# Norm steps and sums of squares on another engine, pool waits by tile, and the norm's row one half block later, in a two-layer decoder trunk

## The chip, the cores and the metric

The kernel runs on one core of one Trainium2 chip. The metric is the device time of one execution in microseconds (us), the median of several runs. The engines are TensorE (PE; PEld is its weight load), VectorE (DVE), ScalarE (ACT), GpSimd (POOL) and SyncE (SP), whose queue issues most loads. SBUF is the memory that all of them work in; PSUM holds what PE accumulates.

## The reference

One sequence of 512 tokens with a width of 1024, in float32, passes two layers. Each layer is a half SwiGLU block, a token mixer and another half SwiGLU block, every one behind an RMS norm and added to the residual:

```
h = h + 0.5 * swiglu(rmsnorm(h, ffn_norm_a[i]), ...)      # hidden width 2816
h = h + mixer_i(rmsnorm(h, mix_norm[i]))                  # layer 0: MLA, layer 1: NSA
h = h + 0.5 * swiglu(rmsnorm(h, ffn_norm_b[i]), ...)
rmsnorm(x, g) = x * rsqrt(mean(x * x) + 1e-6) * g
swiglu(x)     = (silu(x @ w_gate) * (x @ w_up)) @ w_down
```

MLA is multi-head latent attention with 16 heads; NSA is sparse attention with a compressed, a selected and a window branch. A final norm follows. What matters here is the norm: a sum of squares over the 1024 channels for each token, its inverse root, and a product.

## The kernel before

**Layout.** The residual lies in SBUF as eight tiles `h[c]` of 128 channels by 512 tokens. Every matmul is made of three in fp32r, on a high and a low part of both operands: ACT copies the high part, DVE subtracts to get the low part (`split`, L165 to L174; `wslab`, L132 to L155, for weights: L143 the copy, L145 the subtraction on DVE, L149 the subtraction on POOL inside the mixers' attention). Weights pass through two raw buffers (`wr`) and two split ones.

**The norm.** As a chunk of `h` is finished, `norm_chunk` splits it, scaled by the gain only, and `sumsq` (L246) squares it on ACT (L250) and adds the square to `s2` (L254, on POOL). The inverse root is applied late, to the results: `norm_col` (L273) lets PE sum `s2` over the partitions into a column of 128x4 (`pc`, L278) and `rsqrt` (L256) takes its inverse root: three preparing steps on DVE (L259 to L261) and three Newton iterations, of four operations on POOL with `pool=True` (L264 to L267) or of three on DVE without (L269 to L271). `norm_bcast` (L286) spreads the column over all partitions with eight small matmuls (`pb`, L290), and ACT copies that to `row`. The last two chunks ahead of an FFN are kept in `late`; their squares are added inside the FFN. The first FFN takes its sums from a second copy of x, by token (`squares`).

**An FFN** (`ffn`, L368), four of them, works on 22 blocks of 128 hidden channels. The first three (`PLAIN`) are plain matmuls: a gate half (`plain(.., 0, ..)`) and an up half (`plain(.., 1, ..)`) of 48 matmuls of 256 columns each. Their gates need `row`, which is made after the second block: `norm_bcast`, the copy, then `gate` (L374) and `act` for blocks 0 and 1, ahead of the third block's matmuls in the program. `gate` multiplies by `row` on DVE (L377), takes Silu on ACT (L378) and multiplies again (L379). The blocks from 3 on use Strassen's scheme, seven products in place of eight, with sums of weights (`wsums`, on DVE and ACT) and of inputs (`combine`, L224: y on ACT, L236 to L238 and a split on DVE), four combines in each FFN. The products go to `px`, `pq` and `pg` in PSUM; `down` products of the three blocks before are put between them (`unit`). The last four blocks' down product runs chunk by chunk and feeds the next norm.

**The mixers** (`mla`, L641; `nsa`, L833) project, run a software pipeline over tiles of scores (`attend`) and end in an output projection (`w_o`, `po`), whose second half feeds the next norm chunk by chunk. NSA opens further pools on the way: "cmp" for its compressed branch, then "nsat".

**What sets the order.** The framework places semaphores and works out at compile time a fixed order for each engine, from the program's order and from when it expects operands to be ready; every engine's queue then runs in that order. Pools of tiles are stacked in SBUF. An FFN's pools ("act", "ft") and a mixer's pools land on bytes of pools that were released before. By default everything in such a pool waits for every user of those released pools.

Of the kernel before, what the change touches and what calls it, by code (L numbers as in the profile page):

```python
# [15 lines left out]
ALU = mybir.AluOpType  # L16
# [4 lines left out]
D = 1024  # L21
# [40 lines left out]
class Kern:  # L62
# [183 lines left out]
    def sumsq(self, t, first=False):  # L246

        nc = self.nc
        sq = self.sp.tile([P, S], F32, tag="s2", bufs=2, name="s2") if first else self.scratch("sq")
        nc.scalar.activation(sq, t, AF.Square)  # L250
        if first:
            self.s2 = sq
        else:
            nc.gpsimd.tensor_tensor(self.s2, self.s2, sq, op=ALU.add)  # L254

    def rsqrt(self, y, v, t, psum, n, pool):  # L256

# [110 lines left out]
    def ffn(self, idx, gain_next, ap, tp):  # L368
        nc, a = self.nc, self.a
# [4 lines left out]
        def gate(f, g):  # L374

            t = tg[f] = tp.tile([P, S], F32, tag="tg", bufs=2, name="tg")
            nc.vector.tensor_tensor(t, g, row, op=ALU.mult)  # L377
            nc.scalar.activation(t, t, AF.Silu, scale=-1.0)  # L378
            nc.vector.tensor_tensor(t, t, row, op=ALU.mult)  # L379
# [4 lines left out]
        def act(f):  # L384
            t = tu[f]
            if f < PLAIN:
                t = tu_tile()
                nc.vector.scalar_tensor_tensor(t, tu[f], -1.0, tg[f], op0=ALU.mult, op1=ALU.mult)
            else:
                nc.vector.tensor_tensor(t, t, tg[f], op=ALU.mult)  # L390
            ah[f] = ap.tile([P, S], F32R, tag="act", bufs=4 * NG, name="ah")
            al[f] = ap.tile([P, S], F32R, tag="act", bufs=4 * NG, name="al")
            self.split(t, ah[f], al[f])
# [19 lines left out]
        sums, xts = self.small_sums, []  # L413

        def tokens(t):

            xts.append(tp.tile([P, D], F32, tag="fr", bufs=3, name="xt"))
            with self.tc.issue_after(self.high.ins):
                nc.scalar.dma_start(xts[t], a["x_tok"][t * P : (t + 1) * P, :])

        def squares(t):
            nc.scalar.activation(xts[t], xts[t], AF.Square, accum_out=sums[:, t : t + 1])
# [7 lines left out]
        for f, g in enumerate(gates):  # L430
            u = tu[f] = self.bank(("mm", "S")[f % 2], "pu")
            self.plain(idx, f, 0, g)
            if f == 1 and idx == 0:

                squares(0)
                tokens(3)
                squares(1)
            self.plain(idx, f, 1, u)
            if f == 0:
                for c in self.late:  # L440
                    self.sumsq(self.h[c])
                col = self.norm_col(D, self.s2, pool=True) if idx else None
            elif f == 1:
                if idx == 0:
                    squares(2)
                    squares(3)
                    col = self.rsqrt_col(sums, D, pool=True)
                pb = self.norm_bcast(col)
                row = tp.tile([P, S], F32, tag="row", bufs=1, name="row")
                nc.scalar.activation(row, pb, AF.Copy)  # L450
                for e in range(2):
                    gate(e, gates[e])
                    act(e)
            else:
                gate(f, g)
                act(f)
            for p in (((0,), (1,), (2, 3)) if idx else ((0, 1), (2,), (3,)))[f]:
                self.combine(p)
# [182 lines left out]
    def mla(self, gain_next):  # L641
        nc, tc, a = self.nc, self.tc, self.a
        with ExitStack() as cx:
            mp = cx.enter_context(tc.tile_pool(name="mla", bufs=1))
            tp = cx.enter_context(tc.tile_pool(name="mlat", bufs=2))
            self.chain, self.chained = None, True
            self.scr = tp, "p", 6
            cst = mp.tile([P, S], F32, name="cst")
# [184 lines left out]
    def nsa(self, gain_next):  # L833
        nc, tc, a = self.nc, self.tc, self.a
        with ExitStack() as cx:
            mp = cx.enter_context(tc.tile_pool(name="nsa", bufs=1))
            qp = cx.enter_context(tc.tile_pool(name="nsaq", bufs=1))
            rvalid = self.gains[:, 53:57]
            gat = mp.tile([P, 4, 3 * H], F32, name="gat")
            gcmp = mp.tile([P, 4, H], F32, name="gcmp")  # L840
# [91 lines left out]

            ks, vs, qs, pc, th, bank = {}, {}, [], {}, {}, {}

            with tc.tile_pool(name="cmp", bufs=1) as bp:
                self.chain, self.chained = None, True
                bt = self.bias_table(bp)
                for t in vcm:
# [39 lines left out]
                col = self.norm_col(D, self.s2)  # L978
# [36 lines left out]
                    nc.scalar.activation(gat[:, j, :], pv[j][:, 256:VG], AF.Sigmoid, scale=col[:, j : j + 1])  # L1015
                nc.vector.tensor_tensor(gcmp, gat[:, :, 0 : 3 * H : 3], rvalid[:, :, None].to_broadcast([P, 4, H]), op=ALU.mult)

            tp = cx.enter_context(tc.tile_pool(name="nsat", bufs=2))

            pths, ptls = [tp.tile([P, 2 * PTN], F32R, tag=x, bufs=1, name=x) for x in ("npth", "nptl")]  # L1020
            pth, ptl = [[t[:, br * PTN : br * PTN + PTN] for br in range(2)] for t in (pths, ptls)]
# [163 lines left out]
    def run(self):  # L1185
        tc = self.tc
        nxt = ["m0", "b0", "a1", "m1", "b1", "fin"]
        step = 0
        self.begin()
        for layer in range(2):  # L1190
            for which in range(3):
                if which == 1:
                    (self.mla, self.nsa)[layer](nxt[step])
                else:
                    with tc.tile_pool(name=f"act{step}", bufs=1) as ap, tc.tile_pool(name=f"ft{step}", bufs=2) as tp:
                        self.ffn(2 * layer + which // 2, nxt[step], ap, tp)
                step += 1

# [102 lines left out]
```

## Time and profile before

| | |
|---|---|
| median of 3 runs | 1926.41 us (1923.17 to 1928.86) |
| span of the profiled execution, from its first to its last instruction | 1920.1 us |
| PE busy | 1876.1 us (98%) |
| DVE busy | 1518.9 us (79%) |
| ACT busy | 1091.4 us (57%) |
| POOL busy | 334.9 us (17%) |
| mean clock granted to PE | 0.996 |

The profile gives one execution. Its rows name the line, the engine, the operation and the tiles as out<-in; a count is "x8"; square brackets hold the engine's idle time just ahead of an instruction and what ended it. Matmuls overlap, so the number of matmuls in a stretch tells PE's rate better than their durations. Of the execution's own time the profile holds the span; the runs' times are taken around the whole execution and lie some 6 us above it. The spans of the six steps follow from the PE rows: FFN to 347 us, MLA to 562, FFN to 905, FFN to 1249, NSA to 1564, FFN to the end.

### The profile page before, as it was taken

Reading aid. Unit: us, or ns where it says so; the run is one execution under the profiler, and the core shown is the slowest. Engines: PE = TensorE matmul, PEld = TensorE weight load, DVE = VectorE, ACT = ScalarE, POOL = GpSimd, SP = SyncE. Lnnn points to the kernel's source line nnn. Section 1 sums busy time; section 2 is a strip of 40 time slices with the busy share of each in tenths; the row PEclk is TensorE's granted clock in tenths of the full one; section 3 lists DMA queues with packets and bytes.
Section 4 is the critical chain, followed back from the end, with each engine's and each line's share of the span. In section 5 each row is a group of like instructions: output and inputs, shape, how many; then the busy total and the mean of one; then the engine's idle time right before and its main releaser. Section 6 shows DMA issues by size and latency. Waiting matters only on the chain. (4 is left out here: it accounts for less than half of the span.)

```text
span 1920.1 us, 33220 instructions
## 1 busy us (share of the span) xinstructions
PE 1876.1 (98%) x12584; PEld 1707.3 (89%) x12584; DVE 1518.9 (79%) x2838; ACT 1091.4 (57%) x2040; POOL 334.9 (17%) x421
## 2 busy tenths in 40 slices
PE   8999999999999999999999999999999999999998
PEld 8999999878888999998999999877788888999997
DVE  7988886678778888876888888655987978888885
ACT  7555554478665555555555555435877865555553
POOL 1000000257631000002200000114666531000000
PEclk9999999999999999999999999999999999999999
DMA  6433321311233333323333332243122133333321
GB/s 224 140 100 99 113 90 42 110 50 42 73 116 111 100 100 109 112 62 107 117 110 108 104 100 79 65 123 100 51 67 67 40 118 96 108 112 108 104 76 67
DMA packets 75904, 183.28 MB, mean 95 GB/s; under 512 B 9040, under 2 KB 37072, under 8 KB 75744
## 3 DMA queue, kind: packets, MB, share of 16 engines
q1 hardware_dynamic: 72800, 176.39, 29.6%
q10 hardware_dynamic: 2944, 4.77, 0.7%
q8 instruction: 99, 1.62, 0.3%
q14 instruction: 61, 0.50, 0.1%
HBM read 178.96 MB, written 2.16 MB: 94 GB/s over the span
## 5 line engine op out<-in xcount | busy, mean ns | idle before, releaser
L254 POOL TENSOR_TENSOR s<-s,sq 128x512 f32<-128x512 f32 x38 | 55.7, 1466 | 988.2 <-ACT sq L250 985.2
L163 PE MATMUL pd<-al,wd 128*128 128x512 f32 x576 | 225.0, 391 | 0.0
L162 PE MATMUL pd<-ah,wd 128*128 128x512 f32 x576 | 224.8, 390 | 0.0
L164 PE MATMUL pd<-ah,wd 128*128 128x512 f32 x576 | 224.6, 390 | 0.0
L171 DVE TENSOR_TENSOR w<-wr,w 128x1024 fp32r<-128x1024 f32 x72 | 88.1, 1224 | 134.1 <-ACT w L170 134.1
L352 PE MATMUL px<-four,wh 128*128 128x256 f32 x608 | 168.5, 277 | 0.0
L354 PE MATMUL pq<-four,wl 128*128 128x256 f32 x608 | 167.9, 276 | 0.3 <-DVE wl L171 0.3
L354 PE MATMUL px<-four,wl 128*128 128x256 f32 x608 | 168.0, 276 | 0.0
L353 PE MATMUL px<-four,wh 128*128 128x256 f32 x608 | 167.9, 276 | 0.0
L352 PE MATMUL pq<-four,wh 128*128 128x256 f32 x608 | 167.9, 276 | 0.0
L353 PE MATMUL pq<-four,wh 128*128 128x256 f32 x608 | 167.8, 276 | 0.0
L143 ACT ACTIVATE w<-wr 128x1024 fp32r<-128x1024 f32 (+5 forms) x120 | 100.6, 844 | 104.7 <-issue 20.1
L401 DVE SCALAR_TENSOR_TENSOR h<-pd,h 128x512 f32<-128x512 f32 x216 | 148.0, 685 | 13.8 <-PE pd L164 13.7
L170 ACT ACTIVATE wd<-wdr 128x384 fp32r<-128x384 f32 x192 | 99.3, 519 | 101.4 <-ACT wd L170 62.9
L164 PEld LDWEIGHTS pd<-ah,wd 128*128 128x128 f32 x576 | 108.2, 188 | 22.9
L162 PEld LDWEIGHTS pd<-ah,wd 128*128 128x128 f32 x576 | 108.1, 188 | 20.3
L163 PEld LDWEIGHTS pd<-al,wd 128*128 128x128 f32 x576 | 108.1, 188 | 19.7
L145 DVE TENSOR_TENSOR w<-wr,w 128x1024 fp32r<-128x1024 f32 (+4 forms) x81 | 83.3, 1031 | 48.8 <-ACT w L143 48.2
L171 DVE TENSOR_TENSOR wd<-wdr,wd 128x384 fp32r<-128x384 f32 x192 | 105.7, 552 | 18.6 <-ACT wd L170 18.3
L639 ACT ACTIVATE p<-p,small 128x512 f32<-128x512 f32 (+1 forms) x192 | 106.8, 558 | 21.0 <-DVE small L638 17.3
L352 PEld LDWEIGHTS px<-four,wh 128*128 128x128 f32 x608 | 114.1, 188 | 0.9 <-ACT pg L477 0.5
L354 PEld LDWEIGHTS pq<-four,wl 128*128 128x128 f32 x608 | 114.1, 188 | 0.7 <-DVE wl L171 0.7
(359 smaller groups left out, 6281.1 us busy)
## 6 DMA issues: line engine op xcount, KB each, us to landing
wr<-in_w_gu SPq DMA_DIRECT2D x96, 512.0 KB, 3.3
ru<-in_w_gu SPq DMA_DIRECT2D x76, 512.0 KB, 4.2
wdr<-in_w_down SPq DMA_DIRECT2D x192, 192.0 KB, 2.4
wr<-in_w_down SPq DMA_DIRECT2D x24, 256.0 KB, 2.6
wr<-in_mla_w_o SPq DMA_DIRECT2D x8, 512.0 KB, 3.3
wr<-in_nsa_w_q SPq DMA_DIRECT2D x8, 512.0 KB, 3.3
th<-btab_d SPq DMA_DIRECT2D x16, 256.0 KB, 3.6
wr<-in_nsa_w_o SPq DMA_DIRECT2D x8, 512.0 KB, 3.6
```

What stands on the lines that cost most here:

```text
L143: self.copied = nc.scalar.activation(wh[:, m], raw[:, m], AF.Copy)
L145: nc.vector.tensor_tensor(wl[:, m], raw[:, m], f32v(wh[:, m]), op=ALU.subtract)
L162: mm(out, wh, xh, start=first, stop=False)
L163: mm(out, wh, xl, start=False, stop=False)
L164: return mm(out, wl, xh, start=False, stop=last)
L170: nc.scalar.activation(hi, src, AF.Copy)
L171: (nc.gpsimd if pool else nc.vector).tensor_tensor(lo, src, f32v(hi), op=ALU.subtract)
L352: mm(out, wh[:, p], xh, start=first and p == 0, stop=False, skip_group_check=True)
L353: mm(out, wh[:, p], xl, start=False, stop=False, skip_group_check=True)
L354: mm(out, wl[:, p], xh, start=False, stop=last and p == KP - 1, skip_group_check=True)
L401: nc.vector.scalar_tensor_tensor(self.h[c], p, 0.5, self.h[c], op0=ALU.mult, op1=ALU.add)
L639: nc.scalar.activation(p_sb[:, :n], p_sb[:, :n], AF.Exp, bias=nm, scale=-1.0, accum_out=sm)
```

## The change

It has three parts.

1. All additions of `sumsq` go from POOL to DVE, and so do the Newton iterations of the FFNs' norms (`pool=True` is dropped in both calls, so `rsqrt` takes its DVE form of nine operations).
2. `norm_bcast`, the row's copy and the gates and activations of blocks 0 and 1 go from behind the second block's up half to behind the third block's gate half. The sums of the late chunks stay behind the first block, for the FFNs after the first alone.
3. All pools of the FFNs and of both mixers are opened with `reuse_waits="tile"`: a tile waits only for the users of earlier tiles on its own bytes, and not for all users of the pools that lay there.

```diff
@@ sumsq
-            nc.gpsimd.tensor_tensor(self.s2, self.s2, sq, op=ALU.add)
+            nc.vector.tensor_tensor(self.s2, self.s2, sq, op=ALU.add)
@@ ffn, the loop over the three plain blocks
-            self.plain(idx, f, 1, u)
-            if f == 0:
-                for c in self.late:
-                    self.sumsq(self.h[c])
-                col = self.norm_col(D, self.s2, pool=True) if idx else None
-            elif f == 1:
-                if idx == 0:
-                    squares(2)
-                    squares(3)
-                    col = self.rsqrt_col(sums, D, pool=True)
+            if f == 2:
                 pb = self.norm_bcast(col)
                 row = tp.tile([P, S], F32, tag="row", bufs=1, name="row")
                 nc.scalar.activation(row, pb, AF.Copy)
                 for e in range(2):
                     gate(e, gates[e])
                     act(e)
-            else:
+            self.plain(idx, f, 1, u)
+            if f == 0 and idx:
+                for c in self.late:
+                    self.sumsq(self.h[c])
+                col = self.norm_col(D, self.s2)
+            elif f == 1 and idx == 0:
+                squares(2)
+                squares(3)
+                col = self.rsqrt_col(sums, D)
+            elif f == 2:
                 gate(f, g)
                 act(f)
@@ mla, nsa (also "nsaq", "cmp", "nsat") and run (also "ft")
-            mp = cx.enter_context(tc.tile_pool(name="mla", bufs=1))
-            tp = cx.enter_context(tc.tile_pool(name="mlat", bufs=2))
+            mp = cx.enter_context(tc.tile_pool(name="mla", bufs=1, reuse_waits="tile"))
+            tp = cx.enter_context(tc.tile_pool(name="mlat", bufs=2, reuse_waits="tile"))
...
-                    with tc.tile_pool(name=f"act{step}", bufs=1) as ap, ...
+                    with tc.tile_pool(name=f"act{step}", bufs=1, reuse_waits="tile") as ap, ...
```

More of the change, by code (lines that the diff above doesn't have):

```diff
@@ L835, in nsa @@
         with ExitStack() as cx:
-            mp = cx.enter_context(tc.tile_pool(name="nsa", bufs=1))
-            qp = cx.enter_context(tc.tile_pool(name="nsaq", bufs=1))
+            mp = cx.enter_context(tc.tile_pool(name="nsa", bufs=1, reuse_waits="tile"))
+            qp = cx.enter_context(tc.tile_pool(name="nsaq", bufs=1, reuse_waits="tile"))
             rvalid = self.gains[:, 53:57]
@@ L933, in nsa @@
             ks, vs, qs, pc, th, bank = {}, {}, [], {}, {}, {}
-            with tc.tile_pool(name="cmp", bufs=1) as bp:
+            with tc.tile_pool(name="cmp", bufs=1, reuse_waits="tile") as bp:
                 self.chain, self.chained = None, True
@@ L1016, in nsa @@
                 nc.vector.tensor_tensor(gcmp, gat[:, :, 0 : 3 * H : 3], rvalid[:, :, None].to_broadcast([P, 4, H]), op=ALU.mult)
-            tp = cx.enter_context(tc.tile_pool(name="nsat", bufs=2))
+            tp = cx.enter_context(tc.tile_pool(name="nsat", bufs=2, reuse_waits="tile"))
             pths, ptls = [tp.tile([P, 2 * PTN], F32R, tag=x, bufs=1, name=x) for x in ("npth", "nptl")]
@@ L1194, in run @@
                 else:
-                    with tc.tile_pool(name=f"act{step}", bufs=1) as ap, tc.tile_pool(name=f"ft{step}", bufs=2) as tp:
+                    with tc.tile_pool(name=f"act{step}", bufs=1, reuse_waits="tile") as ap, tc.tile_pool(name=f"ft{step}", bufs=2, reuse_waits="tile") as tp:
                         self.ffn(2 * layer + which // 2, nxt[step], ap, tp)
```

## The prediction

> **What bounds the kernel now.** I read the page first: the span, the share of each engine, and the group in which the moved additions stand. TensorE (PE) is busy for all but 44 us of the span (1920.1 - 1876.1). So a change of other engines' work can gain only where PE waits, or where PE runs at a lower clock because it has waited.
>
> ```profile
> span 1920.1 us, 33220 instructions
> PE 1876.1 (98%) x12584; PEld 1707.3 (89%) x12584; DVE 1518.9 (79%) x2838; ACT 1091.4 (57%) x2040; POOL 334.9 (17%) x421
> L254 POOL TENSOR_TENSOR s<-s,sq 128x512 f32<-128x512 f32 x38 | 55.7, 1466 | 988.2 <-ACT sq L250 985.2
> ```
>
> The waits of PE come next (total, number, longest).
>
> ```profile
> PE pb L290 <- POOL small L267: 10.6, 4, 4.2
> PE pcm L164 <- DVE w L145: 2.2, 2, 1.7
> PE ptc L1043 <- issue: 1.7, 1, 1.7
> ```
>
> The largest is the spreading of the norm's row (pb), which waits for the last Newton step on POOL, once in each FFN. PE's order of time gives the four pb waits in the brackets:
>
> ```profile
> 31.64 0.49 PE L290 MATMUL pb<-ident,small 128*128 128x128 f32 x2 [1.11 <-POOL small L267]
> 591.04 0.38 PE L290 MATMUL pb<-ident,small 128*128 128x128 f32 x1 [2.51 <-POOL small L267]
> 932.72 0.38 PE L290 MATMUL pb<-ident,small 128*128 128x128 f32 x1 [2.79 <-POOL small L267]
> 1591.08 0.58 PE L290 MATMUL pb<-ident,small 128*128 128x128 f32 x1 [4.18 <-POOL small L267]
> ```
>
> Why POOL is late is in its own order of time, at the last FFN: the 12 steps begin at 1580.30, and the first one alone, of 4 elements per partition, takes 6.39 us, where the same shape at the end takes 0.20.
>
> ```profile
> 1580.30 6.39 POOL L264 TENSOR_TENSOR small<-small 128x4 f32<-128x4 f32 x1 [9.82 <-DVE small L261]
> 1590.83 0.20 POOL L267 TENSOR_TENSOR small<-small 128x4 f32<-128x4 f32 x1
> ```
>
> **The change part by part. A: pb moves behind a gate half, Newton goes to VectorE (DVE).** A half block is 48 matmuls; this stretch at full clock is one of them:
>
> ```profile
> 597.60:603.20 5.60, 5.60 (x52) 5.60 (x51) 5.00 (x8) 3.34 (x8) 0.00 (x0) 1.00 0.00 0
> ```
>
> So pb is wanted 5.6 us later, and the longest wait is 4.18: even with POOL's timing all four would be covered. With Newton on DVE the steps are also earlier. In the second FFN its preparing step stands at 581.65, among splits that DVE has queued up to 587.9:
>
> ```profile
> 581.65 0.16 DVE L261 TENSOR_SCALAR small<-small 128x4 int32<-128x4 int32 x1
> 586.69 1.22 DVE L145 TENSOR_TENSOR w<-wr,w 128x1024 fp32r<-128x1024 f32 x1
> L271 DVE SCALAR_TENSOR_TENSOR small<-small x12: 161/162/164, 359.8 to 1266.7; 128x4 f32<-128x4 f32 x12
> ```
>
> Nine steps of 0.16 (the last row, min/median/max of the norms that DVE already does) are 1.5 us. At worst each stands behind one of the queued splits, and the column is ready soon after 587.9 + 1.5 = 589.4. In before PE reaches pb at 591.04 - 2.51 = 588.5, in after 5.6 us later, at 594.1. The cover is the gate half itself; if the compiled order left pb ahead of it, 0.9 us (589.4 - 588.5) would be left of this wait. Behind pb stands PE's whole up half, and the steps are chained on DVE alone, so no wait between engines is added. Gain of A: 1.11 + 2.51 + 2.79 + 4.18 = 10.6; bounds 10.6 - 4 x 0.9 = 7.0 and 10.6. The first FFN's loop over late chunks, now left out, is empty there, and MLA's and NSA's norms have their steps on DVE already: nothing for either.
>
> **B: the half clock behind two of these waits.** Stretches cut at the changes of the granted clock (PE, PEld, DVE, ACT, POOL busy with counts, then the clock):
>
> ```profile
> 934.10:937.51 3.41, 3.41 (x19) 3.41 (x18) 2.87 (x5) 1.64 (x3) 0.00 (x0) 0.50 0.26 100
> 937.51:940.92 3.41, 3.41 (x32) 3.41 (x32) 1.61 (x3) 1.23 (x2) 0.00 (x0) 1.00 0.00 0
> 1326.63:1330.05 3.42, 3.12 (x8) 2.58 (x9) 3.19 (x11) 3.06 (x6) 0.47 (x1) 0.50 0.90 329
> 1589.46:1596.29 6.83, 5.21 (x24) 5.21 (x25) 2.48 (x4) 3.03 (x4) 1.32 (x4) 0.50 0.34 109
> ```
>
> The first and the fourth follow the waits of 2.79 and 4.18; the stretch behind the first has 32 matmuls where it had 19. Half of PE's busy time in them is lost: 3.41 / 2 = 1.7 and 5.21 / 2 = 2.6. If the waits go, I take both to go: 4.3; bounds 0 and 4.3. The Trainium skill ("TensorE: Matmul & The Clock Gate", Part 1 on the HAM clock gate) has the clock halve after at least one idle window of about 3.4 us. The trace agrees for the 4.18, but shows a halving behind 2.79 too; by that rule this one has another cause and may stay, and B would be 2.6.
>
> **C: finer waits where the NSA mixer begins.** Today a pool that lands on released bytes waits for all users of the pools that lay there. Two chains show it (q marks a DMA issue):
>
> ```profile
> 1253.56 1.59 POOL L254 TENSOR_TENSOR s<-s,sq 128x512 f32<-128x512 f32 x1 [0.50 <-ACT sq L250]
> 1255.17 0.34 ACTq L819 DMA_DIRECT2D tb<-in_rel_bias  x1
> 1260.09 0.18 DVE L950 COPY xc<-pos 128x16 f32<-128x16 f32 x1 [6.09 <-DMA pos<-in_nsa_pos]
> 1262.42 1.22 DVE L145 TENSOR_TENSOR w<-wr,w 128x1024 fp32r<-128x1024 f32 x1
> 1263.69 0.50 PE L164 MATMUL pcm<-x,w 128*128 128x512 f32 x1 [1.72 <-DVE w L145]
> 1315.25 5.60 POOL L1012 TENSOR_SCALAR vcm<-vc 32x128 fp32r<-32x128 f32 x16 [1.48 <-DVE vc L171]
> 1320.88 1.73 SPq L1031 DMA_DIRECT2D cb<-btab_d  x4
> 1324.60 0.69 DVE L1038 TENSOR_TENSOR e<-sc,cb 128x512 f32<-128x512 f32 x1 [2.46 <-DMA cb<-btab_d]
> 1325.39 0.30 PE L1043 MATMUL ptc<-ident,e 128*128 128x128 f32 x1 [1.70 <-issue]
> ```
>
> The small loads of the "cmp" pool leave ScalarE's (ACT's) queue at 1255.17, just as POOL's last sum ends (1253.56 + 1.59 = 1255.15). DVE stands behind them for 6 us, the weight's split behind DVE, and PE 1.72 behind the split. Later cb leaves when POOL's last copy out of the old pool ends (1315.25 + 5.60 = 1320.85), and PE waits 1.70. With waits by tile the first goes with the earlier load. The second goes unless cb's own bytes are those of vc, which the page doesn't tell. What is late next in the second place is PE's own score matmuls. The half clock at 1326.63 costs 3.12 / 2 = 1.6. Bounds 0 and 1.72 + 1.70 + 1.6 = 5.0; I take both waits and half of the dip, 4.2. SP's later loads, which stand behind cb in its queue, can only come sooner.
>
> **D: the 38 sums on DVE, and the FFN starts.** Where the output projection ends in a norm, POOL's sums and DVE's splits slow each other:
>
> ```profile
> L174 DVE SCALAR_TENSOR_TENSOR x<-h,ngains,x 128x512 fp32r<-128x512 f32 x7 | 8.2, 1186 | 1.6 <-ACT x L173 1.6
> L145 DVE TENSOR_TENSOR w<-wr,w 128x1024 fp32r<-128x1024 f32 x4 | 5.7, 1418 | 0.7 <-ACT w L143 0.5
> L174 DVE SCALAR_TENSOR_TENSOR x<-h,ngains,x x7: 746/752/754, 888.1 to 906.5; 128x512 fp32r<-128x512 f32 x7
> L625 DVE TENSOR_TENSOR h<-po,h x8: 678/680/684, 546.6 to 566.3; 128x512 f32<-128x512 f32 x8
> 546.00:567.00 21.00, 21.00 (x113) 18.12 (x113) 18.61 (x22) 12.61 (x20) 7.17 (x5) 1.00 0.42 120
> ```
>
> The first two rows are of 546 to 568: the split takes 1.19 where the third row, of another norm, has 0.75, and the weight's 1.42 where the row at 586.69 above has 1.22. That is 7 x 0.44 + 4 x 0.20 = 3.9 us of DVE that returns, against 7 sums of 0.68 (a DVE sum of this shape is the row L625), 4.8. The net 0.9 fits in the 2.4 us in which DVE is idle there (21.00 - 18.61): nothing on the path. Queued behind each sum are the next split and PE behind that; if nothing returned, 4.8 - 2.4 = 2.4 us would show at each of three such starts. On the other side a wait goes:
>
> ```profile
> 903.63 0.72 ACT L232 ACTIVATE y<-h,gains 128x512 f32<-128x512 f32 x1 [1.45 <-POOL s L254]
> 906.62 0.39 PE L366 MATMUL pg<-x,w 128*128 128x256 f32 x1 [0.76 <-DVE w L145]
> ```
>
> ACT's first write into the new FFN pool stands 1.45 behind POOL's sum, and the weight's copy behind it, and PE 0.76. I take 0.8; bounds -7.2 and 0.8.
>
> **E: less cover behind pb.** Two gates and activations now have one half block before the first Strassen products, not two. DVE's stretches at the second FFN, and the two instructions that meet:
>
> ```profile
> 592.87:597.70 4.83, 3.78 (x6) 1.00 0.18 70
> 597.70:606.70 9.00, 8.49 (x12) 1.00 0.00 0
> 605.47 1.22 DVE L171 TENSOR_TENSOR wl<-rg,wh 128x1024 fp32r<-128x1024 f32 x1
> 606.80 0.34 PE L354 MATMUL px<-four,wl 128*128 128x256 f32 x1
> ```
>
> The six gate operations (3.78) now fall behind the gate half, into the stretch where DVE already has 8.49 of work until it ends wl at 606.69, just ahead of the product that reads it. From the end of the gate half (597.6) to that product PE needs 9.2 us, with pb 10.1 (an estimate: 8 matmuls at 5.60 / 52 are 0.9). 3.78 + 8.49 - 10.1 = 2.2 late at most, in each of four FFNs: 8.8. At the other end is nothing, since the 12 operations hold work for the following block (its weight split alone is 1.22) that can go behind wl. Nearer to nothing, because the compiled order follows readiness: I take 0.5 each, 2.0.
>
> **Sum.** 10.6 + 4.3 + 4.2 + 0.8 - 2.0 = 17.9. The profiled execution would have a span of 1920.1 - 17.9 = 1902.2. It is 6.3 us under the median of the runs, 1926.4, which holds what lies around the span; the same subtraction gives 1908.5.
>
> **Rivals.** *DVE takes over the wait* (E at its bound, C at 0, D at 0): 10.6 + 4.3 - 8.8 = 6.1, 1920.3. For it: DVE is 94% busy in the stretch before the product (8.49 of 9.00). Against: half of a block's preparation can move ahead of pb, where DVE now idles. *The finer waits do nothing* (bytes that overlap late users, or waits that stay by pool): C and the 0.8 are gone, 1913.5. *The dip at 934 has another cause than the wait*, and its 1.7 stays: 1910.2. For it: behind the wait of 2.51 the clock stayed at 1.00 (592.87:597.70 above). Against: it begins 1.4 us after the wait's end. This is what the skill's rule above would make of it. *Slower: the finer waits let the next FFN's work overtake.* What now stands back behind the pool's wait, above all four combines, could be placed ahead of the weight splits that PE wants at once. A combine has one DVE operation of 1024 elements and three of 512 or fewer: at most 1.22 + 3 x 0.68 = 3.3 by the rows above, 13 for four. Less the 2.4 idle that is 10.6 at each of three starts: 32 us, 1940. It decides the sign from (17.9 + 5.8) / 3 = 8 us at each start. Against it: most of these instructions stand later in the program than the splits.
>
> **How the numbers follow.** 0.3% or 5.8 us is about what can be told from no change, so faster means under 1920.6. Forecast 0.60 (1902 to 1913 by C's and half of E's bounds), DVE's wait 0.17, of which a third ends above 1920.6; idle finer waits 0.12; the dip's other cause 0.05; slower 0.06. Faster 0.60 + 0.11 + 0.12 + 0.05 = 0.88; same 0.06; slower 0.06. The low end takes A, B, C and D at their best and E at nothing: 10.6 + 4.3 + 5.0 + 0.8 = 20.7, and the spread of the runs (5.7, half of it on a median): 1903. I set 1902. The high end holds most of DVE's rival and the idle finer waits: 1920.
>
> **What would show it.** Right: no pb row of PE with a wait over 0.5; POOL without L254 and L264; the granted clock at 1.00 from the first block to the NSA mixer and around the last FFN; pos and cb loaded earlier, and PE's waits of 1.72 and 1.70 gone. E shows as waits of px or pq for wl, and the finer waits as ACT's first y no longer behind a sum. It would be wrong if PE waited for the weight splits (pg, pu behind L145) by more than 8 us at an FFN's start, or if pb still waited.

## The result and the profile after

The changed kernel takes 1899.36 us (1898.70 to 1899.62, 4 runs) where the kernel before takes 1925.87 (1923.17 to 1928.86, 4 runs) on the same chip: a ratio of 0.9866 [0.9849, 0.9883], 26.5 us faster. The forecast was 1908.5 with a range from 1902: the direction was right, the gain was larger than the range allowed by 2.6 us. The profiled execution's span is 1896.9, which is 23.2 under that of before; 17.9 were forecast. So there are two misses: 5.3 us inside the span, and the rest outside that comparison.

The head of the page of after. POOL has lost a fourth of its work, DVE has 10 us more, and PE is busy for all but 28 us of the span (44 before):

```profile
span 1896.9 us, 33129 instructions
PE 1868.7 (99%) x12584; PEld 1701.8 (90%) x12584; DVE 1528.5 (81%) x2912; ACT 1089.9 (57%) x2040; POOL 247.8 (13%) x335
```

PE's waits of after (total, number, longest). The 10.6 of pb behind POOL, the 1.7 of pcm and the 1.7 of ptc behind the late cb are gone. What leads now is the kernel's first weight, which was there before as well; the waits of px are new (1.42 and 0.18):

```profile
PE pg L364 <- ACT w L143: 5.8, 1, 5.8
PE px L352 <- ACT pg L477: 1.6, 2, 1.4
```

PE's order of time has the spreading of the row without a bracket, and DVE's order has the last Newton step of the second FFN at 583.49, 6 us ahead of the matmul that reads it (rows of the first and the second FFN, then DVE's):

```profile
35.61 0.38 PE L290 MATMUL pb<-ident,small 128*128 128x128 f32 x2
589.69 0.27 PE L290 MATMUL pb<-ident,small 128*128 128x128 f32 x1
...
583.49 0.15 DVE L271 SCALAR_TENSOR_TENSOR small<-small 128x4 f32<-128x4 f32 x1
```

Where the 23.2 us went is read from the starts of the same PE rows in both traces: the first matmul into each tile in each step.

| stretch, from one PE row to the next | before | after | difference | forecast |
|---|---|---|---|---|
| first FFN: start to first px | 43.55 | 41.96 | -1.6 | -0.6 (A, E) |
| to the norm column of MLA (346.72, 346.71) | 303.17 | 304.75 | +1.6 | 0 |
| MLA to po (479.93, 478.99) | 133.21 | 132.28 | -0.9 | 0 |
| second FFN: pg (562.39, 561.52) to px (602.95, 596.04) | 40.56 | 34.52 | **-6.0** | -2.0 (A, E) |
| third FFN: px to its pu (912.53, 904.93) | 309.58 | 308.89 | -0.7 | -0.8 (D) |
| its pu to px (946.23, 933.95) | 33.70 | 29.02 | -4.7 | -4.0 (A, B, E) |
| NSA: pcm (1248.79, 1236.72) to po (1466.13, 1449.35) | 217.34 | 212.63 | -4.7 | -4.2 (C) |
| last FFN: pg (1563.93, 1547.18) to px (1605.41, 1581.66) | 41.48 | 34.48 | -7.0 | -6.3 (A, B, E) |

The stretches left out change by +0.1 (MLA's and NSA's po to pg, together), +0.2 (px to pcm) and +0.5 (the last px to the end). The first two rows cancel. The others agree with the forecast within 1 us, but for the second FFN's start, which has 4 of the 5.3.

### The profile page after: what moved, and what is told of

The parts are those of the page before. It is cut to its first block, busy times and chain, and to the rows that moved or that the text cites. A ratio compares the mean times of both kernels' runs of the same rounds, so it can differ in the third digit from the quotient of the medians.

```text
span 1896.9 us, 33129 instructions
## 1 busy us (share of the span) xinstructions
PE 1868.7 (99%) x12584; PEld 1701.8 (90%) x12584; DVE 1528.5 (81%) x2912; ACT 1089.9 (57%) x2040; POOL 247.8 (13%) x335
## 4 chain that ended last, share of the span: by engine, by line
PE 84%; DVE 6%; ACT 5%; issue 2%; POOL 2%; DMA 1%; POOLq 0%; ACTq 0%; SPq 0%; DVEq 0%
PE pd L164 7%; PE pd L163 7%; PE pd L162 7%; PE px L352 5%; PE px L354 5%; PE px L353 5%; PE pg L352 4%; PE pg L354 4%; PE pg L353 4%; PE pq L354 3%; PE pq L352 3%; PE pq L353 3%; ACT p L639 1%; PE o L604 1%; PE pt L593 1%
## 5 line engine op out<-in xcount | busy, mean ns | idle before, releaser
L401 DVE SCALAR_TENSOR_TENSOR h<-pd,h 128x512 f32<-128x512 f32 x216 | 147.4, 683 | 6.9 <-PE pd L164 6.8
L353 PEld LDWEIGHTS pq<-four,wh 128*128 128x128 f32 x608 | 114.1, 188 | 0.1
```

The source lines that it names most:

```text
L353: mm(out, wh[:, p], xl, start=False, stop=False, skip_group_check=True)
L401: nc.vector.scalar_tensor_tensor(self.h[c], p, 0.5, self.h[c], op0=ALU.mult, op1=ALU.add)
```

## The experiments

**What had to be told apart.** Of the span's miss, theory one says: POOL's sums block DVE's splits just when PE waits for these (step D priced them at nothing), so moving the sums away is worth about as much as the pb waits. Its rival: the finer waits or the move of the row do it, and the sums are neutral. Of the miss outside the span, theory one says: the half clock behind PE's waits comes in some executions and not in others, the profiled one was a lucky one, and the change takes away its cause. Its rival: 6 us lie around the span, as the prediction had it.

**The kernel before, unchanged, again.**

> The kernel before, unchanged, to see how its executions differ. Half-clock theory: its median stood 5.8 us above the span of the profiled execution, the changed kernel's 2.5 us, because most executions of before pay for more half-clock stretches behind PE's waits than the profiled one did (two of 3.4 and 6.8 us around FFN starts, one of 3.4 in NSA). Then a new profile of it has a span of 1920 to 1927 with another set of half-clock stretches, and its run's time stays about 2 us above its own span. Rival: the difference lies outside the span (launch, end); then every span is about 1920 and the time above it is 4 to 6 us.

1924.12 us (1921.14 to 1927.05, 10 runs) beside 1924.84 (1920.62 to 1929.53, 13 runs) of the same kernel: a ratio of 0.9996 [0.9986, 1.0007]. Every run's time is its own span plus 1.8 us: 1921.14 has a span of 1919.4 at a mean clock of 0.996, 1929.53 one of 1927.7 at 0.993. So 1.8 us lie around the span, and not 6; the spans themselves differ by 8 us. The windows of this profile, cut where the clock falls to 0.50 (columns as in the prediction), show why:

```profile
33.60:37.00 3.40, 3.40 (x18) 3.40 (x18) 1.62 (x3) 2.43 (x4) 0.00 (x0) 0.50 0.53 159
593.40:596.80 3.40, 3.40 (x18) 3.40 (x18) 1.58 (x3) 2.84 (x4) 0.00 (x0) 0.50 0.48 159
1327.30:1334.10 6.80, 5.81 (x16) 4.75 (x17) 4.82 (x17) 4.59 (x12) 1.70 (x3) 0.50 0.47 183
1593.50:1596.90 3.40, 3.09 (x14) 3.09 (x15) 0.34 (x1) 0.96 (x2) 0.20 (x1) 0.50 0.49 158
```

It is another set than in the first profile. The stretches at 33.6 and 593.4, behind pb waits of 2.51 each, are new; that at 934, behind the third FFN's wait of 2.79, is gone, with the wait still there. The same wait halves the clock in one execution and not in the next. In after the clock is whole until PE's work ends at 1888.8. A mean over so long a row would hide one stretch of 3.4 us, but cut into stretches of 1 us no part of it lies under 1.00 either:

```profile
0.00:1880.00 1880.00, 1859.94 (x12535) 1694.24 (x12536) 1517.92 (x2874) 1084.77 (x2027) 247.82 (x335) 1.00 0.31 97
```

**The move of the row alone** (part 2; steps and sums stay on POOL).

```diff
+            if f == 2:
                 pb = self.norm_bcast(col)
...
+            self.plain(idx, f, 1, u)
+            if f == 0 and idx:
...
+                col = self.norm_col(D, self.s2, pool=True)
```

> The row's spreading behind the third block's gate half, alone; sums and Newton steps stay on POOL, waits stay by pool. Theory: the four pb waits (10.6 us) and the half clock behind them (4.3 in the profile, some more in the median) go even with POOL's timing, since the last step ended at 1591.03 and pb is wanted at 1592.4; E costs about 1.5. The waits at the FFN starts and in NSA stay. 12 to 16 us faster, about 1911. Rival (the steps' engine matters for pb): POOL's steps are pushed back by more DVE work in front, pb waits of 1 to 2 us remain, about 1916.

1905.91 us (1904.49 to 1906.81), 0.9908 [0.9894, 0.9923]. All pb waits of the FFNs go, and no half clock is left ahead of the end. The other waits of PE stay:

```profile
PE ptc L1043 <- issue: 1.6, 1, 1.6
PE pcm L164 <- DVE w L145: 1.6, 1, 1.6
```

So A's first reason holds: the gate half covers the column even with POOL's timing. The 19 us are more than the expectation had, which put the half clock at the profile's 4.3 and some more. The mean clocks of the runs (0.998 here, 0.994 over the 13 of before) make it some 7 us, an estimate: 0.004 of 1925.

**The engines alone** (part 1).

```diff
-            nc.gpsimd.tensor_tensor(self.s2, self.s2, sq, op=ALU.add)
+            nc.vector.tensor_tensor(self.s2, self.s2, sq, op=ALU.add)
...
-                col = self.norm_col(D, self.s2, pool=True) if idx else None
+                col = self.norm_col(D, self.s2) if idx else None
...
-                    col = self.rsqrt_col(sums, D, pool=True)
+                    col = self.rsqrt_col(sums, D)
```

> Sums of squares and Newton steps on DVE, alone; pb at its old place, waits by pool. Theory: pb waits fall to 0 to 0.9 each (DVE's steps end soon after its queue of splits), the FFN starts lose the waits that came from POOL's sums (about 3 us in the profile), half clock behind pb goes: 14 to 19 us faster, about 1909. Rival (the finer waits cleared the FFN starts): those 3 us stay, about 1913, with PE waits for x L174 and w L145 at 568, 583 and 906 as before.

1899.76 us (1899.46 to 1902.77), 0.9881 [0.9866, 0.9895]: nearly the whole change. PE's waits of it, with the row at its old place:

```profile
PE ptc L1043 <- issue: 1.6, 1, 1.6
PE pb L290 <- DVE small L271: 1.1, 3, 0.5
```

With both on DVE, pb is on time in three FFNs at its old place and 0.49 late in the first (the other two of its three waits are in the mixers). One half clock stretch is left, at 1314 behind ptc. The second FFN takes 34.51 us from pg to px (561.80 to 596.31), as in after, and the wait of pcm is gone too.

**The finer waits alone** (part 3: `reuse_waits="tile"` on all pools).

```diff
-            with tc.tile_pool(name="cmp", bufs=1) as bp:
+            with tc.tile_pool(name="cmp", bufs=1, reuse_waits="tile") as bp:
```

> Finer waits alone. Theory: the NSA start loses its 1.72 and 1.70 and its half clock, about 5 us, and the start of the third FFN its 0.76; pb waits stay at 10 to 11: 4 to 7 us faster, about 1920. Rival (the finer waits cleared all FFN starts): 7 to 9 us faster, with no PE wait for x L174 or w L145 at the second and third FFN's starts, about 1918. Rival (early work overtakes the weight splits): PE waits for w L145 grow, same or slower.

1915.72 us (1914.58 to 1917.90), 0.9961 [0.9947, 0.9976], 9 us faster. pcm and ptc no longer wait; pb does as before:

```profile
PE pb L290 <- POOL small L267: 10.7, 4, 4.3
```

From pcm to po it takes 212.53 us (1250.45 to 1462.98), as long as after: C is the work of this part. That is 4.8 of the 9. The two profiled spans differ by 4.0 only (1920.1 and 1916.1), but the one is among the fastest executions of its kernel and the other is the slowest of four. Both hold 13.6 us at half clock ahead of the end, here at 591, 932 and 1587 and no longer in NSA. Over its four runs the mean clock is 0.996, where the 13 of before have 0.994: that is some 4 us, an estimate, and about the rest. The third FFN's start, which the expectation had 0.76 shorter, gained nothing: from px to its pu it takes 309.64 us (309.58 before).

**The Newton steps alone** (the sums stay on POOL).

```diff
-                col = self.norm_col(D, self.s2, pool=True) if idx else None
+                col = self.norm_col(D, self.s2) if idx else None
...
-                    col = self.rsqrt_col(sums, D, pool=True)
+                    col = self.rsqrt_col(sums, D)
```

> Newton steps on DVE alone; sums stay on POOL, pb at its old place, waits by pool. Theory (the sums on POOL, not the steps, make the waits at the FFN starts and MLA's pb wait of 0.59): pb waits and their half clock go, but PE's waits for x L174 and w L145 at the second FFN's start and the 0.59 stay: about 4 us slower than both on DVE, about 1904. Rival (the steps' removal from POOL clears them): same as both on DVE, about 1900.

1910.43 us (1909.95 to 1911.75), 0.9928 [0.9914, 0.9943]. On the same chip the engines together gave 1899.76, so the sums are worth 10.7 of the engines' 25 by the medians, and 9.0 by the ratios: more than twice what was expected. DVE's order of time at the second FFN's start, then POOL's in the same stretch, show how:

```profile
560.19 1.54 DVE L145 TENSOR_TENSOR w<-wr,w 128x1024 fp32r<-128x1024 f32 x1
561.66 1.77 DVE L174 SCALAR_TENSOR_TENSOR x<-h,ngains,x 128x512 fp32r<-128x512 f32 x1
...
567.23 0.74 DVE L174 SCALAR_TENSOR_TENSOR x<-h,ngains,x 128x512 fp32r<-128x512 f32 x1
```

```profile
559.35 1.30 POOL L254 TENSOR_TENSOR s<-s,sq 128x512 f32<-128x512 f32 x1 [2.57 <-ACT sq L250]
561.50 1.38 POOL L254 TENSOR_TENSOR s<-s,sq 128x512 f32<-128x512 f32 x1 [0.85 <-ACT sq L250]
```

The sum that begins at 561.50 ends at 562.88, and the split that DVE began at 561.66 takes 1.77 instead of 0.74: 1.03 lost in one instruction. The weight's split beside the sum at 559.35 has 1.54 instead of 1.22. PE is waiting for just these: it stands 0.32 at 566.99, 0.65 at 568.02 and 0.74 at 582.19, and from pg to px it takes 37.91 us (561.70 to 599.61) where the engines together need 34.51. The other stretches that are longer here are MLA up to po (133.34 and 132.20), NSA from pcm to po (218.59 and 216.06) and the last FFN's start (36.02 and 34.48); the first FFN's start is shorter (36.20 and 37.30). Not all of it is slowed DVE work on PE's path: NSA's 2.5 hold the 1.6 of pcm, which is step C's first chain: the small loads leave ACT's queue at 1247.76, just as POOL's last sum ends at 1247.73.

The group of this split between 540 and 575 in this kernel, and then in the engines alone, sums it up (busy time, mean ns, idle time ahead):

```profile
L174 DVE SCALAR_TENSOR_TENSOR x<-h,ngains,x 128x512 fp32r<-128x512 f32 x8 | 9.0, 1133 | 1.6 <-ACT x L173 1.6
```

```profile
L174 DVE SCALAR_TENSOR_TENSOR x<-h,ngains,x 128x512 fp32r<-128x512 f32 x8 | 5.8, 743 | 0.0
```

Two more rows of DVE in this kernel, of other kinds of operation, and then the sums of POOL that were running as they began:

```profile
372.27 1.26 DVE L261 TENSOR_SCALAR small<-small 128x4 int32<-128x4 int32 x1
888.69 0.69 DVE L401 SCALAR_TENSOR_TENSOR h<-pd,h 128x512 f32<-128x512 f32 x1 [0.48 <-PE pd L164]
```

```profile
371.70 1.81 POOL L254 TENSOR_TENSOR s<-s,sq 128x512 f32<-128x512 f32 x1 [5.12 <-ACT sq L250]
888.02 1.34 POOL L254 TENSOR_TENSOR s<-s,sq 128x512 f32<-128x512 f32 x1 [316.74 <-ACT sq L250]
```

The residual's addition (L401), one of whose inputs comes from PSUM, keeps its 0.69. The preparing step (L261) has one input, in SBUF, and takes 1.26 instead of 0.16, until the sum ends. MLA's pb then waits 0.60 at 375.99, a wait that the engines together don't have: a part of MLA's 1.1.

**The sums alone** (the steps stay on POOL).

```diff
-            nc.gpsimd.tensor_tensor(self.s2, self.s2, sq, op=ALU.add)
+            nc.vector.tensor_tensor(self.s2, self.s2, sq, op=ALU.add)
```

> Sums on DVE alone; Newton steps stay on POOL, pb at its old place, waits by pool. Theory (sums and steps each clear their own waits): the waits for x L174 and w L145 at the second FFN's start and MLA's 0.59 go, pb's four waits stay at 1 to 4 each with their half clock: 8 to 12 us slower than both on DVE, 1908 to 1912. Rival (the sums on POOL also delayed the steps): pb waits fall too, under 1906.

1913.50 us (1911.59 to 1916.33) beside 1927.18 on its chip, 0.9936 [0.9914, 0.9957]. This and the next three ran on another chip than the others, so across them ratios are compared. The waits at the second FFN's start are gone, and its own pb wait with them; the others stay, and the half clock behind two of these:

```profile
PE pb L290 <- POOL small L267: 8.9, 3, 3.3
```

**The sums left out.** On top of the Newton steps alone, the 38 additions are dropped, so the norms see a part of their sum of squares.

```diff
-        else:
-            nc.gpsimd.tensor_tensor(self.s2, self.s2, sq, op=ALU.add)
```

> Newton steps on DVE, and the 38 additions left out altogether (the norms use the first chunk's squares alone, so part of the computation is missing). Shows what the sums cost on DVE: the engines-only kernel minus this. Theory: nothing on the path, since 0.6 us of DVE per chunk fits its idle time: 1899.8 within 1, and no wait at the second FFN's start. Rival (DVE is short at the FFN starts): 2 to 5 us faster than the engines-only kernel.

1901.92 us (1901.08 to 1903.06), 0.9875 [0.9857, 0.9893], where the sums on DVE gave 0.9881 [0.9866, 0.9895]. Having them on DVE costs nothing that can be measured. This half of step D was right: the 26 us of DVE lie in its idle time.

**One more addition on POOL behind each sum.**

```diff
             nc.vector.tensor_tensor(self.s2, self.s2, sq, op=ALU.add)
+            nc.gpsimd.tensor_tensor(sq, sq, sq, op=ALU.add)
```

> The changed kernel with one more addition of the same size on POOL behind each sum on DVE (of the square's tile to itself, used by nothing). Theory (two engines that read SBUF at the same time block each other, and DVE's split is blocked just where PE waits for it): PE waits for x L174 and w L145 come back at the second FFN's start, rows of L174 over 1.5 us appear, 2 to 5 us slower than the changed kernel, about 1903. Rival (POOL was merely the longer link of the chain of sums): no more than 0.5 us slower, 1899.5 to 1900, since nothing reads the new results.

1904.54 us (1902.06 to 1906.07), 0.9887 [0.9867, 0.9906]. Nobody reads what POOL adds here, and waits of PE are back that after doesn't have, such as 0.76 at 903.04 and 0.55 at 575.29:

```profile
PE pg L367 <- DVE w L145: 1.3, 2, 0.8
PE pb L291 <- DVE small L272: 1.1, 3, 0.5
```

DVE's order of time, then POOL's, at the second FFN's start (rows at 561) and the third's (from 893 on):

```profile
560.92 0.74 DVE L174 SCALAR_TENSOR_TENSOR x<-h,ngains,x 128x512 fp32r<-128x512 f32 x1
...
894.07 1.15 DVE L145 TENSOR_TENSOR w<-wr,w 128x512 fp32r<-128x512 f32 x1
...
905.36 2.06 DVE L145 TENSOR_TENSOR w<-wr,w 128x1024 fp32r<-128x1024 f32 x1
```

```profile
561.08 1.48 POOL L255 TENSOR_TENSOR sq<-sq 128x512 f32<-128x512 f32 x1 [2.43 <-DVE s L254]
...
893.62 1.04 POOL L255 TENSOR_TENSOR sq<-sq 128x512 f32<-128x512 f32 x1 [1.89 <-DVE s L254]
904.92 1.42 POOL L255 TENSOR_TENSOR sq<-sq 128x512 f32<-128x512 f32 x1 [4.40 <-DVE s L254]
```

The weight's splits take 1.15 and 2.06 beside POOL's addition (0.69 and 1.22 alone). The expectation had the slowing at the split of `x` (L174) at the second FFN's start; there all eight kept 0.743 on average (one of 1.53 stands at 1550.33). One of them, at 560.92, met POOL's addition, but it was running as that began at 561.08, and kept its 0.74; POOL's took 1.48, where the one at 893.62 has 1.04. So the blocking was shown and the place was missed: it hits DVE operations with two SBUF inputs that begin while POOL's addition runs, though not each of them (L254 at 556.08 kept its 0.68). That POOL was only a longer link in the chain of the sums is out, because nothing depends on this addition. By the ratio it costs 3 to 4 us, and the intervals overlap; the rows carry the verdict.

**After without the finer waits** (parts 1 and 2).

```diff
-            with tc.tile_pool(name="cmp", bufs=1, reuse_waits="tile") as bp:
+            with tc.tile_pool(name="cmp", bufs=1) as bp:
```

> The changed kernel with its pools' waits by pool again. Theory: the wait of 1.6 for ptc in NSA and its half clock, and the third FFN's 0.76, come back, while the wait of 1.72 behind pos stays away since the last sum no longer ends on POOL: 1 to 4 us slower than the changed kernel, about 1902. Rival (the finer waits are worth what they gain alone, 9 us): 1908.

1902.25 us (1901.87 to 1902.55), 0.9876 [0.9855, 0.9897]. ptc waits again, with a half clock at 1313 behind it; pcm does not:

```profile
PE ptc L1043 <- issue: 1.7, 1, 1.7
```

Its span of 1900.6 is 3.7 above after's, 3.8 of it between pcm and po (216.45 and 212.63). The third FFN's 0.76, which was expected back, stays away.

**After, again, without the move, and with the first FFN's row early.** Three on one chip: the changed kernel again; the row back behind the second block in all FFNs (parts 1 and 3); and the row back in the first FFN alone, whose px has the new wait.

```diff
-            if f == 2:
+            if f == 2 and idx:
```

> The changed kernel, unchanged, to have it on the same chip as the next two. 1899.4 within 1, and runs that lie within 1.5 us of each other, since it has no half-clock stretch before its last 10 us.

> The changed kernel with the row's spreading put back behind the second block: sums and Newton steps on DVE, waits by tile. With both on DVE the move alone should be worth nothing, since the engines-only run shows pb waits of 0 in three FFNs and 0.49 in the first. Theory (the move now costs its lost cover): 0.5 to 1.5 us faster than the changed kernel, about 1898.4, without the wait of 1.42 for pg L477 in the first FFN. Rival (the move still gains): pb waits return, 1 to 4 us slower, 1900 to 1903.

> The changed kernel with the row's spreading put back behind the second block in the first FFN alone. Theory: the wait of 1.42 there is exchanged for pb's 0.5: 0.5 to 1 us faster than the changed kernel, about 1898.6. If it equals the version with the move undone in all four, the move is worth nothing in the other three.

1899.56 (1898.63 to 1899.85), 1898.31 (1897.26 to 1898.77) and 1898.95 (1898.33 to 1899.43) us: ratios of 0.9870 [0.9855, 0.9885], 0.9863 [0.9846, 0.9879] and 0.9868 [0.9853, 0.9882]. So the version without the move is the fastest that was measured, by 1.2 us of medians, with ranges that overlap by 0.1. PE's pb waits without the move:

```profile
PE pb L290 <- DVE small L271: 0.7, 2, 0.4
```

Of these, 0.44 is the first FFN's; the other is MLA's and is in after too. So the move buys back 0.44 and pays for it in the same FFN, with the 1.42 of px.

## Why the prediction was right in direction and too small in size

**A, pb** (-10.6): right. All four waits went, and for both reasons given: the move alone clears them, and so do the engines together but for 0.49. Newton on DVE with the sums still on POOL leaves 1.09 in the last FFN (1581.87). Only one of the two was needed.

**B, the half clock** (-4.3): right in the profile. The dips at 934 and 1589 went with the waits. Of the 15 pb waits behind POOL in four traces (before twice, the waits alone, the sums alone) ten have a half clock at them, and none of the ten traces without such waits has one at an FFN's start; the rule of the Trainium skill quoted there would have kept the first dip as one of another cause, and the traces speak against it. But B was taken from one execution, and that is the second miss below.

**C, the finer waits** (-4.2): 4.7 from pcm to po. The two chains were right, but the first has two cures: pcm's wait also goes with the sums on DVE (engines alone, and after without finer waits). The second has one: ptc waits in all kernels that lack finer waits. DMA issues and DVE's first pos row in after show both loads early (1255.17, 1260.09 and 1320.88 in before, while pcm itself came only 12.1 earlier):

```profile
1239.30 0.34 ACTq L819 DMA_DIRECT2D tb<-in_rel_bias  x1
1241.57 0.20 DVE L950 COPY xc<-pos 128x16 f32<-128x16 f32 x1
1299.66 1.81 SPq L1031 DMA_DIRECT2D cb<-btab_d  x4
```

**D, the sums: here the prediction failed.** The step was: "The net 0.9 fits in the 2.4 us in which DVE is idle there: nothing on the path." It added up DVE's work over 21 us and compared it with DVE's idle time over the same 21 us. That tells whether DVE can hold the work, and the run without sums shows that it can. It does not tell what the old sums cost, for POOL blocked DVE inside a chain that PE was waiting for: of the 1.03 us that one split lost, PE had no cover. The rows were in the prediction (1186 against 752 ns), and the waits behind them (0.38, 0.65, 0.22 and 0.78 at the second FFN's start) stood in the trace of before; the step counted the 3.9 us only as relief for DVE. Two of these waits:

```profile
567.78 0.38 PE L364 MATMUL pg<-x,w 128*128 128x256 f32 x1 [0.38 <-ACT x L173]
568.82 0.38 PE L365 MATMUL pg<-x,w 128*128 128x256 f32 x1 [0.65 <-DVE x L174]
```

By the runs the sums on POOL cost 9 to 10.7 us, of which 7.5 stand in the stretches of PE's path named there, and about 1.6 of these are step C's first chain. The Trainium skill ("SBUF — State Buffer", section "Who interferes with whom") has the rule that would have said so: a DVE instruction with two SBUF inputs contends with a GpSimd instruction that reads SBUF, and one with at most one such input, outside DVE's two-port modes, does not. The traces agree with 1.77 against 0.74 for the split, and 0.69 unchanged for the addition with an input from PSUM. The preparing step with one SBUF input (1.26 against 0.16) was slowed all the same, and whether it ran in such a mode no run shows.

**A listed wait is less than what it costs.** This is the other part of the second FFN. Before the 0.78 at 582.99, PE's rows of before are:

```profile
581.94 0.28 PE L365 MATMUL pu<-x,w 128*128 128x256 f32 x1
582.99 0.39 PE L366 MATMUL pu<-x,w 128*128 128x256 f32 x1 [0.78 <-DVE w L145]
583.21 0.28 PE L364 MATMUL pu<-x,w 128*128 128x256 f32 x1
583.33 0.28 PE L365 MATMUL pu<-x,w 128*128 128x256 f32 x1
```

Matmuls of this kind start every 0.114 us in a full stream, but each row lasts 0.28, so the bracket begins 0.17 late; and the first one behind the wait takes 0.22. From start to start the loss is 1.05 + 0.22 - 2 x 0.114 = 1.04. Over the whole start (before, then after; the first column is the time, x the matmuls):

```profile
562.39:606.00 43.61, 39.07 (x330) 37.83 (x328) 36.11 (x51) 27.16 (x39) 12.47 (x15) 1.00 0.38 121
```

```profile
561.52:602.81 41.29, 41.29 (x360) 41.01 (x358) 34.66 (x60) 27.56 (x40) 0.00 (x0) 1.00 0.38 128
```

Before lists 43.61 - 39.07 = 4.5 us of idle time. At after's rate (41.29 / 360) its 330 matmuls need 37.85, so it lost 5.8.

**E, less cover** (-2.0): about right in size, but by luck. It is not 0.5 in each FFN behind DVE's wl, but one wait of 1.42 in the first FFN, and 0.2 in the third. The rows of ACT, then PE, in after:

```profile
45.69 1.04 ACT L170 ACTIVATE wh<-rg 128x1024 fp32r<-128x1024 f32 x1
46.63 0.25 ACT L461 ACTIVATE gains<-pg,gains 128x1 f32<-128x1 f32 x1
46.78 0.38 ACT L477 ACTIVATE pg<-px 128x256 f32<-128x256 f32 x1
```

```profile
47.21 0.39 PE L352 MATMUL px<-four,wh 128*128 128x256 f32 x1 [1.42 <-ACT pg L477]
937.95 0.39 PE L352 MATMUL px<-four,wh 128*128 128x256 f32 x1 [0.18 <-ACT pg L477]
```

It is ACT that is late, with its copy of the first product out of PSUM behind a weight's copy of 1.04, and not DVE's wl. The wait of 1.42 stands behind that FFN's first px, so the first row of the table shows A's gain and the second this loss, and the two cancel.

**The sum's base.** "It is 6.3 us under the median of the runs, 1926.4, which holds what lies around the span": this was wrong. 1.8 us lie around it; the profiled execution would have shown 1921.9, 4.5 under the median of its runs, as one of the fastest of a kernel that varies by 8 us with the half clock. The change takes away most of that variation (its 4 runs lie within 0.9 us), so it gains those 4.5 less the 0.7 by which its own profiled execution lies under its median. With the 5.3 of the span that makes the miss of 9.1.

**The rivals.** None came. DVE did not take over the wait (wl is not what px waits for), the finer waits did work, and no combine overtook the splits: where the finer waits stand alone, the starts of the second and the last FFN keep their length within 1 us. The parts' gains alone (19, 25 and 9 us) add up to twice the whole, mainly because two waits (pb's, with the half clock behind them, and pcm's) each have two cures; that sum was not taken apart further.

## What to carry to other kernels

When two engines slow each other, don't set the busy time that comes back against idle time: look at whether the slowed instruction is one that the bound engine is waiting for, and price it there. Before a profiled span is taken as the base, compare the spans and mean clocks of the runs; if the clock halves behind short waits in some of them, a change that removes those waits earns more at the median than one profile shows. When two edits aim at the same wait, try each alone: here the move was not needed once the engines had changed.

## What the runs showed of the hardware that was not expected

- The granted clock halves for 3.4 or 6.8 us behind PE waits of 2.5 us (593.4 in the second profile of before) and behind the 1.5 to 1.7 of ptc with shorter waits beside it (0.42 and 0.56 in before): in six of the eight traces that have ptc's wait (from 1311 to 1327) and in none of the six that lack it. So the same wait does it in one execution and not in another. The Trainium skill ("TensorE: Matmul & The Clock Gate", Part 1 on the HAM clock gate) asks for an idle window of about 3.4 us; these runs show it behind less.
- POOL's and DVE's operations do not slow each other evenly. A DVE operation with two SBUF inputs that begins while POOL's runs can lose most of what POOL's still has to run (1.03 of the 1.22 us from 561.66 to 562.88, 0.84 of the 0.98 from 905.36 to 906.34). One that was running first keeps its time (0.74 at 560.92), and so does one with an input from PSUM (0.69 at 888.69). A step of 128x4 with one SBUF input lost 1.10 (1.26 at 372.27), which no run here explains.
- A PE wait costs about 0.3 us more than its bracket (1.04 for 0.78), so many short ones weigh more than their list.
